# The opening of a hybrid decoder block: two projection units from un-normalised rows, in a written order

## The chip, the cores and the metric

The kernel runs on one core of a Trainium2 chip. The metric is the device time of one execution in microseconds (us); lower is better. The engines are TensorE (PE in the profile, its weight loads PEld), VectorE (DVE), ScalarE (ACT), GpSimd (POOL) and SyncE (SP), whose queue issues every DMA here.

## The reference, cut to what matters

One layer on 2048 positions of 1024 channels in float32: a norm, one combined input projection, two token mixers side by side (gated linear attention and a short gated convolution), an output projection, and a gated feed-forward part. The change concerns the norm and the first columns of the input projection.

```python
h = rmsnorm(x, norm1_g)                 # x * rsqrt(mean(x*x) + eps) * g, per position
proj = h @ w_in                         # columns: q, k, v, g, a (gate rank 16), conv B, C, h
q, k = p_q * DK ** -0.5, p_k            # 4 heads of 64
gate_logits = p_a @ w_gate_up + b_gate  # the forget gate, from the 16 columns a
log_a = log_sigmoid(gate_logits) / 16
```

The norm multiplies each position by one factor, so (x * g) @ w times the position's factor is the same as rmsnorm(x, g) @ w.

## The kernel before, in words

**Layout.** Activations lie transposed: channels on 128 partitions, positions along the free axis, in blocks of 512 positions (block j = 0 and 1 make the first half, 2 and 3 the second). A matmul has a 128x128 piece of weights and 128x512 positions. Every operand of a matmul is split into two float32r parts: hi, which ScalarE copies, and the remainder lo, which VectorE subtracts (`split`, L162 to L165). A product of two split operands is three matmuls: hi by hi, lo by hi, hi by lo.

**Units.** The input projection has 12 units for each half. A unit has 256 columns of `w_in`, so with two blocks of positions and two halves of channels a 2x2 by 2x2 block product. From unit 2 on it is done with seven products in place of eight (`PRODUCTS`, L36): weights A11, S1, S2, A12, S3, S4, A22 against activations B11, T1, T2, B21, T3, B22, T4, where S1 to S4 are sums and differences of weight quarters and T1 to T4 those of the normalised activations (`unit`, L452). Each product is 12 matmuls. The results accumulate in PSUM banks that are used on: the first product's bank `oa` is copied out into c11, takes the third product, is copied into c12, takes the fifth, is added into c22 and takes the seventh. The mixtures of the weights are made by GpSimd (L430 to L432, L437). Four buffers hold split weights, two hold raw weights, 28 hold operands, and eight PSUM banks serve all.

**The opening.** `first_loads` (L567) loads block 0's rows in halves, unit 0's four weight quarters, block 1's rows, and block 1 already transposed (`xt`). TensorE turns block 0's rows (32 transposes, L599), ScalarE takes their squares (L595). The squares' sums give one factor for each position by logarithm, exponential and a Newton step (`rsqrt`, L167); `rows_rstd` (L540) copies each factor over 128 columns (L552), and TensorE turns that (four transposes, L555) into a bank that holds the factors along the free axis. `scaled` (L613) multiplies a turned block by gain and factors, and the result is split. `build_first` (L322) does units' first work: for j = 0 and 1 and for each of 8 channel groups k, one normalised operand and six matmuls (two result rows, L362 to L364). `plain_unit` (L385) does unit 1 with the plain eight block products. Units 0 and 1 together take 192 matmuls. `differences` (L366) makes T1 to T4 from the normalised operands, which are overwritten.

**The gate.** `gate` (L691) multiplies 16 columns of `w_in` with the block: 32 matmuls into one bank (L702), then copies of it (a_sb, L713 to L715), the second factor `wgu_sb`, four matmuls (L724) and `forget_gate` (L730) with four running sums on VectorE each time. It is background work: a list of generators from which `tick` takes one step after each product (L241), paced by `pause(8)`. Behind it stand row statistics of the second half (`row_stats`, L517) and `h1_ahead` (L646), which prepares that half's operands.

**What sets the order.** The program is written in one order, and a scheduler with a timeline moves instructions of an engine past each other where dependences allow; `tc.issue_after` forces one instruction behind another. Within an engine the built order is strict. SP's DMAs are issued in its queue's order.

Of the kernel before, what the change touches and what calls it, by code (L numbers as in the profile page):

```python
# [52 lines left out]
def tile_hymba_block(ctx, tc, x, xt, win, wa, wgu, wout, wffn, wdown, wdown_first, small, out):  # L53
# [98 lines left out]
    second_weights, unit_splits, unsplit = [], [], []  # L152
# [8 lines left out]

    def split(src, hi, lo):  # L162
        last_hi[:] = [act.activation(hi, src, AF.Copy)]  # L163
        last_lo[:] = [dve.tensor_tensor(lo, src, hi.bitcast(F32), ALU.subtract)]  # L164
        return last_lo[0]  # L165
# [95 lines left out]
    def pause(n):  # L261
        for _ in range(n):
            yield

# [57 lines left out]
    def build_first(quad, w):  # L322


        ops = {b: [] for _, b in PRODUCTS}
        h, o = {}, {}
        quarters = ("A11", "A12"), ("A21", "A22")
        los = []

        def weight(n, i, *marks):  # L330
            with ExitStack() as stack:
                for m in (last_exp[0], *marks):
                    stack.enter_context(tc.issue_after(m.ins))
                w[n] = weight_quarter(first_raw[0][:, i, :])

        weight("A11", 0, last_copy[0])
        los.append(last_lo[0])
        for j in range(2):
            for r in range(2):
                o[r, j] = bank()  # L340
            for k in range(KD):
                with tc.issue_after(los[-2 if len(los) > 2 else -1].ins):
                    h[k, j] = quad(k, j)
                if (j, k) == (0, 0):
                    weight("A21", 3, last_scaled[0])
                x = opp.tile([P, 2, PB], F32R, name="op", tag="op")
                los.append(split(h[k, j][:], x[:, 0, :], x[:, 1, :]))
                hi = last_hi[0]
                if j == 0 and k in (1, 2):
                    weight(*(("A12", 1), ("A22", 2))[k - 1], los[-1])  # L350
                if j == 0 and k < PT:
                    with tc.issue_after(hi.ins):
                        row_squares(k)
                if (j, k) == (0, PT + 2):
                    rbs[1] = rows_rstd(squares[1][:, :, 0])
                name = ("B11", "B12")[j] if k < 4 else ("B21", "B22")[j]
                ops.setdefault(name, []).append(x)
                c = slice(k % 4 * P, (k % 4 + 1) * P)
                for r in range(2):
                    q = w[quarters[r][k // 4]]  # L360
                    with tc.issue_after(last_turn[0].ins):
                        pe.matmul(o[r, j][:], q[:, 0, c], x[:, 0, :], start=k == 0, stop=False)  # L362
                    pe.matmul(o[r, j][:], q[:, 1, c], x[:, 0, :], start=False, stop=False)
                    pe.matmul(o[r, j][:], q[:, 0, c], x[:, 1, :], start=False, stop=k == KD - 1)  # L364

        def differences(wanted):  # L366
            for n, y, a, b in (
                ("T1", (0, 0), (0, 1), (0, 0)), ("T2", (0, 0), (4, 1), (0, 0)),
                ("T3", (0, 1), (4, 1), (0, 1)), ("T4", (0, 0), (4, 0), (0, 0)),
            ):  # L370
                for k in range(4 if n in wanted else 0):
                    yy, aa, bb = [h[k + dk, j] for dk, j in (y, a, b)]
                    with tc.issue_after(los[-1].ins):
                        dve.tensor_tensor(yy[:], aa[:], bb[:], ALU.subtract)
                    o = opp.tile([P, 2, PB], F32R, name="op", tag="op")
                    ops[n].append(o)
                    if n == "T4":
                        unsplit.append((yy, o))
                    else:
                        with behind(second_weights):  # L380
                            split(yy[:], o[:, 0, :], o[:, 1, :])

        return ops, [(r, j, o[r, j], True) for j in range(2) for r in range(2)], differences

    def plain_unit(src, ops, differences):  # L385

        raw = raw_weights(src)
        us, columns = [], (("B11", "B21"), ("B12", "B22"))
        w = [weight_quarter(raw[:, i, :]) for i in (0, 1, 3, 2)]
        second_weights[:] = last_hi + last_lo  # L390
        differences(("T1", "T2", "T3"))
        for r in range(2):
            for j in range(2):
                o = bank()
                for i, n in enumerate(columns[j]):
                    for k in range(4):
                        product_step(o, w[2 * r + i], ops[n], k, i == 0)
                    tick()
                us.append((r, j, settled(o, True), False))
        return us  # L400

    halves = []

    def weight_quarter(src):

        n = src.shape[-1]
        if halves:
# [44 lines left out]
    def unit(src, ops, into=None, onto=None, raw=None):  # L452
# [19 lines left out]
        def plus(t, o):  # L472
            dve.tensor_tensor(t[:], o[:], t[:], ALU.add)  # L473
            return t
# [913 lines left out]
```

## Time and profile before

| what | value |
| --- | --- |
| timed runs | median 2060.56 us (2060.33, 2060.56, 2063.51) |
| the profiled execution | span of 2059.3 us; the page lists no other time of it |
| PE busy | 2018.4 us, 98% |
| DVE busy | 1425.3 us, 69% |
| ACT busy | 959.7 us, 47% |
| POOL busy | 859.8 us, 42% |
| HBM | 274.98 MB read, 144.70 MB written |

The span runs from the first to the last instruction on the core. A row of a timeline gives start, duration, engine, line, operation, written and read tile, shapes and count, and in brackets the idle time before it with what ended it. A row of a table by stage gives the stage, its length, and for PE, PEld, DVE, ACT and POOL the busy time and the count. A matmul's duration overlaps its neighbours'; the time from one start to the next is its cost in a stream.

### The profile page before, as it was taken

The page shows a single profiled execution, that of the slowest core. Times are in us where ns is not written, and L with a number is a line of the kernel's source. Part 1 is how long each engine was busy: PE and PEld are TensorE (multiplying, and loading weights), DVE is VectorE, ACT ScalarE, POOL GpSimd, SP SyncE. Part 2 cuts the span into 40 slices and gives each one's busy share as a digit, 9 for nine tenths or more (in the row PEclk, how much of TensorE's full clock was granted, in tenths as well). Part 3 has the DMA queues.
Part 4 walks back from the last instruction along what each step waited for, and adds up shares of the span by engine and source line. Part 5 has one row for each costly group of instructions (what it writes and reads, how often), then busy time and mean ns, then how long its engine had stood idle before and what let it go on. Part 6 is the DMA issues. An engine that isn't in the chain of part 4 may idle for free.

```text
span 2059.3 us, 27063 instructions
## 1 busy us (share of the span) xinstructions
PE 2018.4 (98%) x9229; PEld 1657.3 (80%) x9229; DVE 1425.3 (69%) x2128; ACT 959.7 (47%) x1918; POOL 859.8 (42%) x622
## 2 busy tenths in 40 slices
PE   7999999999999999999999999999999999999997
PEld 6877888787888888888888878787888888878786
DVE  8789686559743886676675676767666666667774
ACT  6655365765542344444444452334434444453344
POOL 0345322122102564464564345534644544435544
PEclk9999999999999999999999999999999999999998
DMA  6378485416586873545454676476444434586653
GB/s 229 116 274 278 159 319 165 143 67 194 190 296 246 311 254 130 198 181 207 156 185 143 241 264 254 185 282 257 163 164 167 175 140 169 179 309 223 234 217 126
DMA packets 188729, 421.47 MB, mean 205 GB/s; under 512 B 19792, under 2 KB 65072, under 8 KB 178992
## 3 DMA queue, kind: packets, MB, share of 16 engines
q1 hardware_dynamic: 188592, 419.76, 57.2%
q8 instruction: 72, 1.18, 0.2%
q14 instruction: 65, 0.53, 0.1%
HBM read 274.98 MB, written 144.70 MB: 204 GB/s over the span
## 4 chain that ended last, share of the span: by engine, by line
PE 84%; DVE 7%; DMA 4%; ACT 3%; issue 1%; POOL 1%; SPq 0%; DVEq 0%; ACTq 0%; POOLq 0%
PE mm L448 24%; PE mm L449 23%; PE mm L450 23%; PE mm L945 3%; PE mm L948 3%; PE mm L946 3%; DVE wq L164 2%; DVE op L164 1%; DMA op<-sa_B 1%; DMA op<-sa_T 1%; PE a_ps L702 1%; ACT wq L163 1%; DMA siT<-lo 1%; PE o_ps L869 1%; PE o_ps L871 1%
## 5 line engine op out<-in xcount | busy, mean ns | idle before, releaser
L448 PE MATMUL mm<-op,wq 128*128 128x512 f32 x2499 | 973.7, 392 | 10.3 <-ACT c L480 5.3
L449 PE MATMUL mm<-op,wq 128*128 128x512 f32 x2499 | 972.5, 390 | 1.6 <-DVE op L164 1.6
L450 PE MATMUL mm<-op,wq 128*128 128x512 f32 x2499 | 961.3, 390 | 2.6 <-DVE wq L164 2.3
L164 DVE TENSOR_TENSOR wq<-raw,wq 128x512 fp32r<-128x512 f32 (+2 forms) x626 | 508.9, 818 | 262.6 <-ACT wq L163 260.0
L163 ACT ACTIVATE wq<-raw 128x512 fp32r<-128x512 f32 (+2 forms) x626 | 364.9, 589 | 585.6 <-PE mm L450 447.9
L448 PEld LDWEIGHTS mm<-op,wq 128*128 128x128 f32 x2499 | 468.9, 188 | 114.9 <-ACT c L480 8.0
L450 PEld LDWEIGHTS mm<-op,wq 128*128 128x128 f32 x2499 | 469.1, 188 | 103.8 <-DVE wq L164 6.1
L449 PEld LDWEIGHTS mm<-op,wq 128*128 128x128 f32 x2499 | 469.3, 188 | 99.1 <-DVE op L164 3.7
L432 POOL TENSOR_TENSOR raw<-s,raw 128x512 f32<-128x512 f32 (+2 forms) x97 | 133.3, 1374 | 518.5 <-DVE wq L164 474.7
L430 POOL TENSOR_TENSOR s<-raw 128x512 f32<-128x512 f32 (+2 forms) x97 | 127.4, 1313 | 247.5 <-DMA raw<-in_wffn_dram 90.7
L473 DVE TENSOR_TENSOR c<-mm,c 128x512 f32<-128x512 f32 x198 | 135.8, 686 | 72.7 <-PE mm L450 70.9
L473 DVE TENSOR_TENSOR y<-mm,y 128x512 f32<-128x512 f32 x185 | 126.9, 687 | 83.3 <-PE mm L450 82.9
L437 POOL TENSOR_TENSOR raw<-raw 128x512 f32<-128x512 f32 (+2 forms) x97 | 120.6, 1244 | 126.7 <-DVE wq L164 126.7
L927 POOL TENSOR_TENSOR ssx<-ssx,q 128x512 f32<-128x512 f32 x52 | 77.4, 1504 | 158.8 <-ACT q L926 158.5
L431 POOL TENSOR_TENSOR raw<-raw 128x512 f32<-128x512 f32 (+2 forms) x97 | 137.3, 1416 | 4.9
L480 ACT ACTIVATE c<-mm 128x512 f32<-128x512 f32 x198 | 116.1, 587 | 11.1 <-PE mm L450 9.3
L945 PE MATMUL mm<-op,wq 128*128 128x512 f32 x256 | 100.9, 395 | 0.0
L946 PE MATMUL mm<-op,wq 128*128 128x512 f32 x256 | 99.7, 389 | 0.0
L163 ACT ACTIVATE wq<-s 128x512 fp32r<-128x512 f32 (+2 forms) x97 | 56.9, 587 | 89.3 <-PE mm L450 85.4
L164 DVE TENSOR_TENSOR wq<-s,wq 128x512 fp32r<-128x512 f32 (+2 forms) x97 | 82.6, 852 | 2.8 <-ACT wq L163 2.1
L164 DVE TENSOR_TENSOR op<-op 128x512 fp32r<-128x512 f32 x94 | 76.8, 844 | 4.7 <-ACT op L163 4.6
L948 PE MATMUL mm<-op,wq 128*128 128x512 f32 x256 | 79.8, 390 | 0.0
(204 smaller groups left out, 1807.6 us busy)
## 6 DMA issues: line engine op xcount, KB each, us to landing
raw<-in_wffn_dram SPq DMA_DIRECT2D x44, 1024.0 KB, 6.5
sa_B<-so SPq DMA_DIRECT2D x47, 512.0 KB, 4.2
op<-sa_B SPq DMA_DIRECT2D x47, 512.0 KB, 7.1
raw<-in_win_dram SPq DMA_DIRECT2D x23, 1024.0 KB, 5.4
sa_T<-so SPq DMA_DIRECT2D x44, 512.0 KB, 4.5
op<-sa_T SPq DMA_DIRECT2D x44, 512.0 KB, 6.9
raw<-in_wdown_dram SPq DMA_DIRECT2D x24, 768.0 KB, 5.8
sx<-y SPq DMA_DIRECT2D x48, 256.0 KB, 4.0
```

The costliest lines, as they stand in the source:

```text
L163: last_hi[:] = [act.activation(hi, src, AF.Copy)]
L164: last_lo[:] = [dve.tensor_tensor(lo, src, hi.bitcast(F32), ALU.subtract)]
L430: pool.tensor_tensor(s1, a21, a22, ALU.add)
L431: pool.tensor_tensor(a21, a11, a21, ALU.subtract)
L432: pool.tensor_tensor(a11, s1, a11, ALU.subtract)
L448: pe.matmul(o[:], wh, xh, start=first and k == 0, stop=False, skip_group_check=True)
L449: pe.matmul(o[:], wh, xl, start=False, stop=False, skip_group_check=True)
L450: return pe.matmul(o[:], wl, xh, start=False, stop=k == n - 1, skip_group_check=True)
L473: dve.tensor_tensor(t[:], o[:], t[:], ALU.add)
L945: pe.matmul(o[e, j][:], wh, m[:, 0, :], start=k == 0, stop=False)
L946: pe.matmul(o[e, j][:], wh, m[:, 1, :], start=False, stop=False)
L948: pe.matmul(o[e, j][:], wl, ops[k][j][:, 0, :], start=False, stop=k == KD - 1)
```

## The change

The opening is written anew as one function, `opening`, whose instructions on ScalarE and VectorE stand in a given order (`queued` forces each behind the one before it on its engine; a remainder is queued after the next hi part).

- Block 0 of units 0 and 1 is computed from the turned rows times the gain, without the position's factor: `taken` splits straight from PSUM (ScalarE scales by the gain; VectorE's remainder is one scalar_tensor_tensor). The factor is applied to the results on VectorE (`out` with j = 0).
- Their second block follows, from normalised operands, then the gate's 32 matmuls, then unit 2.
- Twelve matmuls on a tile of ones are issued before the transposes.
- Loads are in another order: unit 0's first two weight quarters come ahead of the second halves of the rows, unit 1's weights are loaded in quarters, and block 0's lower channel groups are also loaded transposed (four more loads).
- Normalised operands of block 0 are made after those of block 1; T1 comes ahead of the gate's product, T2 ahead of unit 2's weights, T3 and T4 among them (`between`).
- Unit 2's mixtures of weights are made by VectorE in the given order, and its additions are issued behind the last instruction of this order (`given`).
- `pause`, `build_first`, `plain_unit`, `first_loads` and `build_h` go; `rows_rstd` keeps the variant without tables, in two steps.

```diff
+    def queued(eng, issue):
+        with behind([tails[eng]] if eng in tails else []):
+            tails[eng] = issue()
+        return tails[eng]
+    def catch_up():
+        while late:
+            last_lo[:] = [queued(dve, late.pop(0))]
...
+        last_hi[:] = [queued(act, lambda: act.activation(hi, src, AF.Copy, scale=scale))]
+        catch_up()
...
+                lambda: dve.scalar_tensor_tensor(lo, src, gain, top, ALU.mult, ALU.subtract)
...
+        def mix(*args):
+            if ordered:
+                queued(dve, lambda: dve.tensor_tensor(*args))
+            else:
+                pool.tensor_tensor(*args)
...
+        w = unit_weights(src, raw, between)
+        given = []
+        if ordered:
+            catch_up()
+            ordered.clear()
+            given += last_lo
...
-            dve.tensor_tensor(t[:], o[:], t[:], ALU.add)
+            with behind(given):
+                dve.tensor_tensor(t[:], o[:], t[:], ALU.add)
...
+        for t in range(PT):
+            fetch_rows(0, t, 0)
+        fetch_w(0, 0)
+        fetch_w(0, 3)
+        for t in range(PT):
+            fetch_rows(0, t, 1)
+        fetch_w(0, 1)
+        fetch_w(0, 2)
+        fetch_w(1, 0)
...
+        def taken(k):
+            x_op[k] = opp.tile([P, 2, PB], F32R, name="op", tag="op")
+            split_in_order(xts[k][:], x_op[k][:, 0, :], x_op[k][:, 1, :], col(C_G1 + k))
...
+            if j:
+                queued(act, lambda: act.activation(c[:], acc[:], AF.Copy))
+            else:
+                queued(dve, lambda: dve.tensor_tensor(c[:], acc[:], rb0[:], ALU.mult))
...
+        for _ in range(12):
+            pe.matmul(warm[:, 0:P], ones[:], ones[:], start=True, stop=True)
+        turned(0)
+        for t in range(PT):
+            square(0, t, 0)
+        weight(0, "A11")
+        taken(0)
+        weight(0, "A21")
+        taken(1)
+        square(0, 0, 1)
+        taken(2)
+        square(0, 1, 1)
+        taken(3)
+        for k in range(3):
+            for r in range(2):
+                mark = column(0, 0, r, k)
+        with behind([mark]):
+            turned(1)
+        weight(0, "A12")
+        square(0, 2, 1)
+        taken(4)
+        weight(0, "A22")
+        taken(5)
+        square(0, 3, 1)
+        est = estimate(0)
+        taken(6)
+        for k in range(3, 6):
+            for r in range(2):
+                mark = column(0, 0, r, k)
+        weight(1, "A11")
+        rep = spread(*est)
+        taken(7)
+        rb_ps, done = turn(rep, mark)
...
+        after = []
+        steps = gate(0, ops, mark, after)
+        next(steps)
+        made("T2")
+        between = [
+            [lambda: out(1, 1, 0)], [lambda: out(1, 1, 1)], [partial(made, "T3"), lambda: after.extend(last_hi)], [],
+            [partial(made, "T4")],
+        ]
+        return ops, raw2, between, steps
```

More of the change, by code (lines that the diff above doesn't have):

```diff
@@ L320, in combine @@
             yield
[L322 to L400, printed above, removed]
@@ L1250, in tile_hymba_block @@
     act.preload_act_table_set("natural_log_exp_and_others")
-    first_loads()
-    for i in range(6):
-        load(carry[16 * i : 16 * i + 16, 0:2, :], wgu[0:16, :].rearrange("p (h c) -> p h c", c=P))
-    ops, first, differences = build_h()
+    ops, raw, between, steps = opening()
     hurry.append(True)
```

374 lines of the change are left out of this document (266 added, 108 removed).

## The prediction

> **What bounds the kernel now.** I read the totals first, then the busy time by stage (columns: busy time and count of PE, PEld, DVE, ACT and POOL, then granted clock, DMA share, GB/s), then the timeline of the opening, engine by engine.
>
> ```profile
> span 2059.3 us, 27063 instructions
> PE 2018.4 (98%) x9229; PEld 1657.3 (80%) x9229; DVE 1425.3 (69%) x2128; ACT 959.7 (47%) x1918; POOL 859.8 (42%) x622
> ```
>
> ```profile
> 0.00:28.30 28.30, 17.06 (x75) 13.96 (x76) 19.27 (x47) 18.98 (x42) 1.11 (x7) 0.94 0.88 315
> 28.30:111.00 82.70, 82.70 (x365) 67.91 (x363) 66.88 (x119) 52.18 (x112) 23.24 (x11) 1.00 0.39 137
> 111.00:210.00 99.00, 95.47 (x419) 77.28 (x419) 86.22 (x128) 51.60 (x101) 53.23 (x36) 1.00 0.79 270
> 210.00:2059.00 1849.00, 1823.15 (x8375) 1498.20 (x8373) 1252.95 (x1836) 836.92 (x1664) 782.19 (x569) 1.00 0.57 203
> ```
>
> TensorE is the bound: busy 2018.4 of 2059.3 us. Of the 40.9 us in which it is idle, 28.3 - 17.06 = 11.2 lie ahead of 28.3 us, none from there to 111, 3.5 from 111 to 210 and 25.9 in the rest, where TensorE's order is the same in both built programs but for a few places. In the second stage 365 matmuls fill 82.7 us: 0.2266 us each. So the change can win only in the first 28 us, and it loses wherever it opens a gap behind them. Why TensorE starts late:
>
> ```profile
> 5.08 1.94 PE L599 MATMUL xt<-ident,xr 128*128 128x128 f32 x8 [5.08 <-DMA xr<-in_x_dram]
> 7.29 4.04 PE L599 MATMUL xt<-ident,xr 128*128 128x128 f32 x24 [0.28 <-DMA xr<-in_x_dram]
> 13.32 0.64 PE L555 MATMUL rb_ps<-ident,rep 128*128 128x128 f32 x4 [1.98 <-DVE rep L552]
> 16.39 0.73 PE L362 MATMUL mm<-op,wq 128*128 128x512 f32 x1 [2.42 <-ACT op L163]
> ```
>
> ```profile
> 7.33 0.63 ACT L595 ACTIVATE q<-xr 128x512 f32<-128x512 f32 x1 [0.94 <-DMA xr<-in_x_dram]
> 7.87 0.19 ACT L595 ACTIVATION_READ_ACCUMULATOR q<-xr 128x1 f32 x1
> 7.99 0.63 ACT L595 ACTIVATE q<-xr 128x512 f32<-128x512 f32 x1
> ...
> 11.88 0.21 ACT L169 ACTIVATE rl<-msq 128x4 f32<-128x4 f32 x1 [0.43 <-DVE msq L543]
> 12.12 0.21 ACT L170 ACTIVATE ry<-rl 128x4 f32<-128x4 f32 x1
> 12.23 2.18 ACT L163 ACTIVATE wq<-raw 128x512 fp32r<-128x512 f32 x4
> 14.31 0.58 ACT L611 ACTIVATE rb<-rb_ps 128x512 f32<-128x512 f32 x1
> 15.70 0.63 ACT L163 ACTIVATE op<-h 128x512 fp32r<-128x512 f32 x1 [0.81 <-DVE h L615]
> ```
>
> The transposes of the rows run from 5.08 us as the rows land (ScalarE's third square waits until 7.33, the fourth follows at 7.99). The first matmul comes at 16.39: it needs an operand that is already normalised, so it stands behind all squares, logarithm and exponential (11.88, 12.12), the row factors and the first split (15.70). The weights' splits, at 12.23, are earlier.
>
> **The change, step by step.** Times are on the trace's axis; durations and pitches are those of the rows; the orders on the engines are those of the two built programs.
>
> ```profile
> 12.35 0.16 DVE L175 TENSOR_TENSOR rl<-ry 128x4 f32<-128x4 f32 x1 [0.51 <-ACT ry L170]
> 12.55 0.16 DVE L176 SCALAR_TENSOR_TENSOR rl<-rl,msq 128x4 f32<-128x4 f32 x1
> 12.75 0.16 DVE L177 SCALAR_TENSOR_TENSOR msq<-rl,ry 128x4 f32<-128x4 f32 x1
> 12.95 0.63 DVE L552 COPY rep<-msq 128x128 f32<-128x128 f32 x4
> 13.49 0.69 DVE L164 TENSOR_TENSOR wq<-raw,wq 128x512 fp32r<-128x512 f32 x1
> ```
>
> ```profile
> 14.00:16.00 2.00, 0.00 (x0) 0.00 (x0) 1.26 (x3) 1.19 (x3) 0.00 (x0) 1.00 1.04 414
> 16.00:18.00 2.00, 1.61 (x4) 1.33 (x5) 1.90 (x4) 1.62 (x4) 0.00 (x0) 0.62 1.01 396
> 18.00:20.00 2.00, 2.00 (x6) 1.51 (x6) 1.96 (x4) 2.00 (x5) 0.00 (x0) 0.53 1.06 388
> 20.00:22.00 2.00, 2.00 (x11) 1.62 (x10) 2.00 (x4) 2.00 (x4) 0.00 (x0) 1.00 1.05 386
> ```
>
> *First matmul.* The operands are now the turned rows times the gain, split straight from PSUM, and two quarters of the weights are fetched in places 5 and 6, behind the four half rows. At 414 GB/s 256 KB take 0.63 us; the fourth is there by 7.99, so these land at about 8.6 and 9.3. ScalarE's splits follow each other at (2.18 - 0.63)/3 = 0.52, its squares at 7.99 - 7.33 = 0.66. The fourth square is over at 8.7; then weight 8.7, operand 9.2 to 9.8, second weight 9.7, second operand 10.2. VectorE's remainders (0.69 each) start behind them at 9.3, 9.9, 10.6 and 11.2. First matmul at 9.85, 6.5 us earlier. 18 matmuls then run almost without a gap: 14.1.
>
> *Up to the first row factors.* 16 more transposes follow. Four turns took 0.64 us with the drain of the last (13.32); I take 2.0 for the 16, which gives 16.1 (2.6 at most). The fifth operand is split from 15.85, then a weight, the sixth operand (0.52 each) and the last square with its sum (0.66 + 0.19): 18.15. Sum and mean 0.4, logarithm and exponential 0.21 each with gaps: 19.05. The seventh operand's split and remainder: 20.4. Newton's three steps at 0.2, the copies from 21.0, the first turn 0.37 later (12.95 to 13.32): 21.35. TensorE has 18 matmuls meanwhile, to 20.2, and **waits 1.15 us**.
>
> ```profile
> 27.95 0.64 PE L555 MATMUL rb_ps<-ident,rep 128*128 128x128 f32 x4 [1.48 <-DVE rep L552]
> 28.35 0.48 PE L362 MATMUL mm<-op,wq 128*128 128x512 f32 x1
> ```
>
> What follows the turns starts 0.40 behind their start, at 21.8; the 12 last matmuls of unit 0's first block end at 24.5. Before: at 28.35 eight turns and 36 of these 48 matmuls were done, and 12 more make 31.07. After: 24.5 with four turns, the other four are due later: 25.15. **Gain of the opening 5.9 us.**
>
> *To the gate's product.* Still 144 matmuls and four turns: 24.5 + 32.6 + 0.64 = 57.8, if they are fed.
>
> ```profile
> 28.63 1.41 DVE L615 SCALAR_TENSOR_TENSOR h<-h,sml,rb_ps 128x512 f32<-128x512 f32 x2 [0.42 <-PE rb_ps L555]
> ...
> 41.09 4.90 DVE L374 TENSOR_TENSOR h<-h 128x512 f32<-128x512 f32 x8
> ...
> 63.66 1.23 DVE L164 TENSOR_TENSOR wq<-raw,wq 128x512 fp32r<-128x512 f32 x1 [1.85 <-ACT wq L163]
> ```
>
> ```profile
> 69.43 3.01 PE a_ps L702 x13
> ...
> 75.18 4.42 PE a_ps L702 x19
> ```
>
> A normalised operand costs VectorE 0.67 + 0.60 = 1.27 us (pitches in the rows at 28.63 and 41.09); TensorE spends 6 x 0.2266 = 1.36 on it. The first is complete at 35.9, TensorE comes at 36.0: it holds, by 0.1 at first and by more later. The operands of the first block and T1 are ready at 55.2. The gate's 32 matmuls take 3.01 + 4.42 = 7.4, as before: 65.2.
>
> *The new wait.* Unit 2 has seven products of 12 matmuls, 2.72 us each. The last, A22 with T4, accumulates into a bank that the addition into c22 must first have read, and this addition is now made to issue behind A22's remainder, the end of the given order. In the built order of before, the next unit's first product and the start of its second stand ahead of this one and hide the addition; in that of after nothing does. ScalarE's queue is in order, and c22's copy in it waits for the second product: 65.2 + 5.45 + 0.25 = 70.9. Behind it stand two squares and then T3's third split, which ends at 73.3. From there VectorE has 18 instructions of 0.60 in its given order, the addition into c22 the last: 10.8 us, with 0.6 of waits for ScalarE's splits 84.7. TensorE is there at 65.2 + 6 x 2.72 = 81.5. **Cost 3.2 us** (1.5 if half of ScalarE's queue and VectorE's waits dissolve, 4.5 if GpSimd, below, collides with it).
>
> *After it.* The forget gate's work on VectorE now starts behind this wait, some 4 us later against TensorE's place than before, and ScalarE's copy of unit 2's last result holds its queue until that product is done. Laid against TensorE's through units 3 and 4, VectorE's order delivers remainders 0.05 to 0.8 us before they are needed. Nothing is left for a collision with GpSimd:
>
> ```profile
> 54.12 8.83 POOL L432 TENSOR_TENSOR raw<-s,raw 128x512 f32<-128x512 f32 x1 [20.35 <-DVE wq L164]
> 63.03 1.30 POOL L430 TENSOR_TENSOR s<-raw 128x512 f32<-128x512 f32 x1
> ```
>
> A remainder took 1.23 us in place of 0.69 beside GpSimd's addition at 63.03, and GpSimd's own took 8.83 in place of 1.30 beside a busy VectorE. Four additions that each cost VectorE 0.54 make 2.2. Bounds 0 and 2.2; I take 1.0, the middle, since TensorE's wait in unit 2 lets VectorE catch up.
>
> *Costed at nothing.* The twelve warming matmuls lie ahead of 5.08, where TensorE is idle (eight cold transposes took 1.94, so 12 make 2.9 us if it were not). VectorE's extra work (eight remainders of un-normalised operands, four scalings of outputs, unit 2's four mixtures from GpSimd, less four copies: 12 x 0.60 to 0.67, about 7.7 us) fits into the 82.7 - 66.9 = 15.8 us that it had free up to 111; without that cover all of it would come out on TensorE. SP issues four more loads of 256 KB (2.5 us), wanted only at 45 us.
>
> **Sum:** -5.9 + 3.2 + 1.0 = -1.7 us on the span of 2059.3, so 2057.6. The timed runs' median, 2060.56, stands 1.26 above that span, which I carry over: **2058.9**.
>
> **The rivals.** *The wait in unit 2 is mostly hidden* and VectorE keeps up, with 1.2 us left of both: -5.9 + 1.2, so 2055.9. For it: ScalarE's chain is laid from rows of other stages; against it: the instruction order shows the dependence. *The clock is cold* at the first matmuls: the stages at 16 and 18 us show half the clock (0.62, 0.53) after TensorE had idled, and full clock from 20. If the warming matmuls and transposes don't count, some 3.4 us at half rate cost 1.7: 2060.6. Against it: TensorE is busy for most of each stretch from 1.2 us on. The Trainium skill, "TensorE: Matmul & The Clock Gate", Part 1, says that the gate watches a free-running window of 3413 ns, so that the slow stretch ends at another place from run to run; the trace's slow rows agree with that length. *The opening starts later than laid*, because a weight's landing or the row factors come 3 us late: -2.9 + 4.2, so 2061.9. *VectorE becomes the bound through units 3 and 4* (slower): GpSimd's eight mixtures of these units each hold it for their 1.3 us while it is the late one, 10.4 us, less some 2 that it makes up: -5.9 + 3.2 + 8.4, so 2066.3. It decides once VectorE's work for a unit exceeds the unit's 84 x 0.2266 = 19.0 us; from 111 to 210 it was busy 86.2 of 99, or 16.6 for each unit, which speaks against it. The Trainium skill, "SBUF — State Buffer", section "SBUF: two separate sides", calls the ports that these two engines share an exclusive lock for a whole instruction; the 1.23 and the 8.83 agree.
>
> **How the numbers follow.** Forecast 2058.9 with chance 0.45, hidden wait 0.22, cold clock 0.12, late opening 0.08, VectorE as the bound 0.13. This measurement can tell about 0.2%, or 4.1 us, from no change: 2056.4 to 2064.7 counts as the same. So faster 0.22, same 0.65, slower 0.13. The range takes in the forecast with its bounds and the first three rivals and leaves out the last: from 2055.4 (the hidden wait with 0.5 us less of it) to 2063.1 (the late opening with 2.2 in place of 1.0).
>
> **What would show it.** The first matmul near 9.9 us; a gap of about 1 us before the first turns of row factors; TensorE without a gap from 22 to 81 us; a gap of about 3 us ahead of unit 2's last product, ended by VectorE's addition into c22; small gaps, ended by VectorE's remainders, up to 112. If the granted clock is half at 10 us, or the gap in unit 2 is missing or exceeds 5 us, the sum is wrong there.

## The result and the profile after

| | before | after |
|---|---|---|
| time, median of 6 runs | 2061.31 us (2059.86 to 2063.51) | 2067.57 us (2064.27 to 2070.10) |
| ratio | | 1.0029, 95% interval 1.0017 to 1.0041 |
| profiled execution: time, span | 2060.56, 2059.3 us | 2064.27, 2062.5 us |

The changed kernel is slower, by about 6 us. The forecast was 2058.9, faster than before, with a range up to 2063.1: it had the wrong sign, and the measured time lies above the range. The profiled execution of the changed kernel is the shortest of its six; the traces of the experiments repeat what it shows up to 213 us, but only in part what it gains after that.

First the page's totals and the busy time by stage (PE, PEld, DVE, ACT, POOL with counts, then granted clock, DMA share, GB/s), cut at the same times as before the change:

```profile
span 2062.5 us, 27137 instructions
```

```profile
0.00:28.30 28.30, 23.72 (x114) 19.55 (x115) 14.42 (x33) 18.39 (x40) 1.11 (x7) 0.94 0.92 320
28.30:111.00 82.70, 78.88 (x342) 64.13 (x341) 76.12 (x137) 53.32 (x112) 9.44 (x7) 0.98 0.41 134
111.00:210.00 99.00, 93.61 (x406) 74.47 (x405) 83.24 (x129) 51.42 (x102) 53.24 (x36) 1.00 0.80 270
210.00:2062.00 1852.00, 1827.88 (x8397) 1502.18 (x8395) 1256.87 (x1846) 837.90 (x1670) 784.59 (x569) 1.00 0.57 203
```

Up to 28.3 us TensorE did 114 matmul records where it did 75; 24 of the 114 are the warming ones (the twelve leave two records each). In the second stage, where it had no idle time at all, it now idles 82.70 - 78.88 = 3.8 us, and VectorE's busy time there rose from 66.88 to 76.12. To see where the time went I numbered TensorE's matmuls from the end of both traces (the changed one has 24 more in all, at its start) and took, for the same place of the order, the start after less the start before:

| place, time before | 34 us | 79 | 89 | 93 | 129 | 138 | 164 | 178 | 192 | 199 | 206 | 220 | 553 | 2050 |
|---|---|---|---|---|---|---|---|---|---|---|---|---|---|---|
| after less before, us | -3.2 | -3.6 | +0.8 | +1.4 | +4.2 | +3.7 | +0.1 | +0.1 | +2.2 | +4.6 | +5.8 | +6.0 | +6.0 | +3.2 |

A gain of 3.6 us at the opening; a loss of 5.0 around 84 to 91 us; 2.3 more by 138 (only 0.6 of it by 112, where the difference is +2.0); 3.6 given back by 164, where the kernel before has gaps of its own; then 5.9 lost from 178 to 220. From there to 553 us nothing changes.

The opening, TensorE's timeline after (start, length, engine, line, operation, count, idle time before it and what ended it):

```profile
1.12 4.88 PE L709 MATMUL warm<-ones 128*128 128x128 f32 x24 [1.12 <-DVE ones L79]
5.84 2.49 PE L598 MATMUL xt<-ident,xr 128*128 128x128 f32 x16
10.33 0.51 PE L686 MATMUL mm<-op,wq 128*128 128x512 f32 x1 [2.00 <-ACT op L178]
...
13.97 0.63 PE L687 MATMUL mm<-op,wq 128*128 128x512 f32 x1
...
15.81 0.40 PE L686 MATMUL mm<-op,wq 128*128 128x512 f32 x1
...
23.86 0.64 PE L652 MATMUL rb_ps<-ident,rep 128*128 128x128 f32 x4 [1.12 <-DVE rep L642]
```

ScalarE's first split, of the weight that the first matmul needs:

```profile
9.07 0.63 ACT L178 ACTIVATE wq<-raw 128x512 fp32r<-128x512 f32 x1 [0.56 <-DMA raw<-in_win_dram]
```

The first matmul stands at 10.33 (16.39 before). Between about 12 and 15.5 us a matmul takes 0.63 instead of 0.39 us and they start 0.43 apart instead of 0.23: half clock. The turns of the row factors come at 23.86.

Unit 2's end, TensorE and then VectorE:

```profile
83.83 0.39 PE L414 MATMUL mm<-op,wq 128*128 128x512 f32 x1
87.57 0.76 PE L412 MATMUL mm<-op,wq 128*128 128x512 f32 x1 [3.35 <-DVE c L443]
88.14 0.63 PE L413 MATMUL mm<-op,wq 128*128 128x512 f32 x1
...
90.63 0.39 PE L413 MATMUL mm<-op,wq 128*128 128x512 f32 x1
```

```profile
83.43 0.68 DVE L677 TENSOR_TENSOR h<-h 128x512 f32<-128x512 f32 x1
84.03 1.47 DVE L182 TENSOR_TENSOR op<-h,op 128x512 fp32r<-128x512 f32 x2
85.42 0.69 DVE L182 TENSOR_TENSOR wq<-raw,wq 128x512 fp32r<-128x512 f32 x1
86.14 1.89 DVE L443 TENSOR_TENSOR c<-mm,c 128x512 f32<-128x512 f32 x3
```

The wait that was forecast is there, with its length (3.35 us) and its releaser, and matmuls at half clock follow it up to 90.3. VectorE runs without a break ahead of it: differences, remainders, then the additions.

How full VectorE is shows in windows of 60 to 90 us and three later ones, first of the kernel before, then after:

```profile
60.00:90.00 30.00, 30.00 (x133) 24.59 (x132) 16.67 (x25) 16.48 (x34) 10.57 (x7) 1.00 0.29 101
93.00:112.00 19.00, 18.79 (x83) 15.24 (x82) 17.81 (x44) 15.43 (x41) 3.05 (x2) 1.00 0.58 201
141.00:178.00 37.00, 34.36 (x149) 27.45 (x148) 32.14 (x36) 17.51 (x31) 25.42 (x17) 1.00 0.98 343
178.00:213.00 35.00, 34.33 (x150) 27.75 (x150) 34.49 (x46) 18.10 (x39) 14.67 (x11) 1.00 0.70 221
```

```profile
60.00:90.00 30.00, 26.65 (x112) 21.38 (x111) 27.71 (x42) 18.62 (x38) 3.57 (x3) 0.95 0.20 60
93.00:112.00 19.00, 18.53 (x82) 14.93 (x81) 18.79 (x39) 16.74 (x41) 5.60 (x4) 1.00 0.61 197
141.00:178.00 37.00, 37.00 (x165) 30.64 (x164) 29.02 (x37) 18.87 (x32) 23.79 (x17) 1.00 0.94 318
178.00:213.00 35.00, 30.13 (x125) 22.53 (x124) 33.83 (x44) 17.93 (x39) 19.19 (x12) 1.00 0.75 245
```

From 60 to 90 us VectorE (the third pair) was busy 16.67 of 30 us before and is busy 27.71 now. In the kernel before that was no idle time thrown away: there VectorE ran ahead. I call *lead* the time from the end of a weight's remainder to the first matmul that reads it (the n-th remainder laid beside the n-th product in the trace). Before, the last four weights of unit 2 had leads of 13.3, 14.2, 14.3 and 12.0 us; after, 5.7, 1.4, 2.1 and 2.5. What held VectorE back there in the kernel before is seen in its longest wait and in ScalarE's just before it:

```profile
75.88 0.69 DVE L164 TENSOR_TENSOR wq<-raw,wq 128x512 fp32r<-128x512 f32 x1 [4.99 <-ACT wq L163]
```

```profile
75.22 0.63 ACT L163 ACTIVATE wq<-raw 128x512 fp32r<-128x512 f32 x1 [4.57 <-PE mm L450]
```

VectorE waited for the hi part of a weight, and ScalarE could write that only when TensorE had done a product: the split weights were as far ahead as their buffers allow. This lead is spent by the end of unit 3, whose seven weights have leads from 7 us down to about 4 before, and from 3 to 6 after. From unit 5 on the two kernels have much the same, between about 1 and 8 us.

### The profile page after: what moved, and what is told of

Same layout as the page of the kernel before. It is cut to its first block, busy times and chain, and to the rows that moved or that the text cites. A ratio compares the mean times of both kernels' runs of the same rounds, so it can differ in the third digit from the quotient of the medians.

```text
span 2062.5 us, 27137 instructions
## 1 busy us (share of the span) xinstructions
PE 2024.1 (98%) x9253; PEld 1660.3 (81%) x9253; DVE 1430.6 (69%) x2140; ACT 961.0 (47%) x1922; POOL 848.4 (41%) x618
## 4 chain that ended last, share of the span: by engine, by line
PE 86%; DVE 7%; DMA 2%; ACT 2%; issue 1%; POOL 1%; SPq 0%; DVEq 0%; ACTq 0%; POOLq 0%
PE mm L412 24%; PE mm L414 24%; PE mm L413 24%; PE mm L1131 3%; PE mm L1132 3%; PE mm L1134 3%; DVE wq L192 2%; DMA op<-shT 1%; PE a_ps L890 1%; PE mm L688 1%; PE mm L686 1%; PE mm L687 1%; PE o_ps L1055 1%; PE o_ps L1057 1%; DVE op L192 1%
## 5 line engine op out<-in xcount | busy, mean ns | idle before, releaser
L412 PE MATMUL mm<-op,wq 128*128 128x512 f32 x2467 | 962.6, 393 | 14.9 <-ACT c L450 6.8
L413 PE MATMUL mm<-op,wq 128*128 128x512 f32 x2467 | 960.4, 390 | 0.3 <-DVE op L192 0.2
L414 PE MATMUL mm<-op,wq 128*128 128x512 f32 x2467 | 949.6, 390 | 4.3 <-DVE wq L192 4.2
L192 DVE TENSOR_TENSOR wq<-raw,wq 128x512 fp32r<-128x512 f32 (+2 forms) x612 | 495.3, 814 | 255.0 <-ACT wq L191 252.5
L191 ACT ACTIVATE wq<-raw 128x512 fp32r<-128x512 f32 (+2 forms) x612 | 355.6, 587 | 575.8 <-PE mm L414 441.3
L412 PEld LDWEIGHTS mm<-op,wq 128*128 128x128 f32 x2467 | 463.3, 188 | 120.0 <-ACT c L450 10.4
L414 PEld LDWEIGHTS mm<-op,wq 128*128 128x128 f32 x2467 | 463.3, 188 | 105.5 <-DVE wq L192 8.5
L413 PEld LDWEIGHTS mm<-op,wq 128*128 128x128 f32 x2467 | 463.7, 188 | 95.6 <-DVE op L192 1.8
L386 POOL TENSOR_TENSOR raw<-s,raw 128x512 f32<-128x512 f32 (+2 forms) x96 | 124.1, 1293 | 503.5 <-DVE wq L192 465.3
L1131 PE MATMUL mm<-op,wq 128*128 128x512 f32 x256 | 100.9, 395 | 0.0
L1132 PE MATMUL mm<-op,wq 128*128 128x512 f32 x256 | 99.7, 390 | 0.0
L1134 PE MATMUL mm<-op,wq 128*128 128x512 f32 x256 | 79.7, 390 | 0.0
L1326 POOL TENSOR_TENSOR y<-x,y 128x512 f32<-128x512 f32 x32 | 53.7, 1678 | 44.7 <-DVE y L443 40.4
```

The costliest lines, as they stand in the source:

```text
L386: pool.tensor_tensor(*args)
L412: pe.matmul(o[:], wh, xh, start=first and k == 0, stop=False, skip_group_check=True)
L413: pe.matmul(o[:], wh, xl, start=False, stop=False, skip_group_check=True)
L414: return pe.matmul(o[:], wl, xh, start=False, stop=k == n - 1, skip_group_check=True)
L1131: pe.matmul(o[e, j][:], wh, m[:, 0, :], start=k == 0, stop=False)
L1132: pe.matmul(o[e, j][:], wh, m[:, 1, :], start=False, stop=False)
```

## The experiments

Every time is the median of 4 to 12 runs, beside the kernel before on the same chip.

**1 to 4: the forced wait, the later h1 operands, the warming.** The first theory was that three separate things lose the time: the order behind the remainder (*wait*), the later start of the second half's operands h1, whose first difference on GpSimd came at 141.1 us instead of 133.0 (*late mixes*), and the cold clock.

```diff
 e1:             ordered.clear()
-            given += last_lo
+            pass
 e2:                 dve.tensor_copy(rep[:, t, :], y[:, t : t + 1].to_broadcast([P, P]))
-        yield
         rb.append(bank("rb_ps"))
 e3:
-        warm = bank("warm")
-        for _ in range(12):
-            pe.matmul(warm[:, 0:P], ones[:], ones[:], start=True, stop=True)
```

> The changed kernel, with the additions of unit 2 no longer placed behind the last remainder of its weights (the list that forces it is left empty). The changed kernel stood 6.3 us over the kernel before. Theory 'wait': the gap of 3.35 us before A22's product (83.84 to 87.57) goes, and with it the half clock at 87.1 to 90.6 that follows it; the matmul that stood 0.8 us later than before at 89 us stands about 3.6 us earlier, and all of the 4.4 us reach the end: about 1.9 us over the kernel before. Rival 'swallowed': at 164 to 178 us both kernels stood level (0.1 us apart) although they were 4 us apart just before, so a later wait levels them; the gap goes, but the end stays within 1.5 us of the changed kernel, about 6 us over the kernel before.

> The changed kernel, with the row factors of blocks 2 and 3 made in one background step each, as before, not in two (one yield of two left out). Theory 'late mixes': the two more steps start the h1 mixes on GpSimd 8 to 10 us later (first one at 141.1 against 133.0, last at 199.0 against 189.3), so they run beside units whose VectorE work they stretch to 1.77 us a piece, and this makes the 5.8 us lost between 178 and 213 us: the mixes end near 189 us, the loss there falls to under 2 us, and the kernel stands about 2 us over the kernel before (4 us under the changed kernel). Rival 'debt': the loss comes from VectorE work carried over from units 2 to 4, wherever the mixes stand: still 5 us or more over the kernel before.

> The changed kernel without the 12 small warming matmuls ahead of the first transposes. In the changed kernel they run from 1.12 to 6.00 us and push the first transposes from 5.08 to 5.84. Theory 'landing': the first product waits for weight A11 to land (9.05 us), for ScalarE's copy of it (9.07) and for the first operand (op hi at 9.61), so the transposes' 0.8 us are cover and the first matmul stays within 0.3 us of 10.33; the transposes run at half clock from 5.1 and the clock windows move by some us; end within 1 us of the changed kernel. Rival 'warm': without them the first products run at half clock for one window of 3.4 us more, 1.7 us later by 20 us.

> The edits of e1_no_given and e2_one_step together. If 'wait' and 'late mixes' both hold and their losses are apart in time, the two gains add: 8 us under the changed kernel, about 2 us under the kernel before, with neither the gap at 84 us nor the loss between 178 and 213 us. If the early gain is levelled by a later wait (rival 'swallowed'), the time is that of e2_one_step alone to within 1 us.

| | median | kernel before | ratio, 95% interval |
|---|---|---|---|
| e1, additions not placed behind the remainder | 2066.20 | 2061.54 | 1.0022, 1.0013 to 1.0032 |
| e2, one step per block | 2068.12 | 2061.54 | 1.0029, 1.0019 to 1.0038 |
| e3, no warming matmuls | 2067.79 | 2061.54 | 1.0023, 1.0012 to 1.0035 |
| e4, e1 and e2 | 2066.04 | 2061.54 | 1.0026, 1.0017 to 1.0035 |

None brings the loss back. In e1 the gap does not go, it shrinks by 0.6 us and changes its releaser (TensorE's timeline):

```profile
86.79 0.50 PE L412 MATMUL mm<-op,wq 128*128 128x512 f32 x1 [2.33 <-ACT wq L178]
88.01 0.79 PE L414 MATMUL mm<-op,wq 128*128 128x512 f32 x1 [0.44 <-DVE wq L182]
```

and this is why, on VectorE and then on ScalarE:

```profile
84.86 0.69 DVE L677 TENSOR_TENSOR h<-h 128x512 f32<-128x512 f32 x1
85.47 0.69 DVE L443 TENSOR_TENSOR c<-mm,c 128x512 f32<-128x512 f32 x1
86.07 1.29 DVE L182 TENSOR_TENSOR op<-h,op 128x512 fp32r<-128x512 f32 x2
87.27 0.69 DVE L182 TENSOR_TENSOR wq<-raw,wq 128x512 fp32r<-128x512 f32 x1
```

```profile
85.58 0.63 ACT L178 ACTIVATE op<-h 128x512 fp32r<-128x512 f32 x1 [0.57 <-DVE h L677]
86.12 0.61 ACT L178 ACTIVATE wq<-raw 128x512 fp32r<-128x512 f32 x1
```

The additions now come earlier, and what stood behind them comes later: T4's last difference ends at 85.55 us, ScalarE's splits of T4 and of A22 follow it, and A22's remainder ends at 87.96, not 86.11. The order decides only which of the results that hang on VectorE is the last one. So "wait" falls as a cause. In e2 TensorE loses nothing from 164 to 206 us (6.2 us behind the kernel before at 164 and from 178 to 192, 6.6 at 206), but it has already lost the same by 164: "late mixes" falls as well. e3's first matmul came at 9.99 us, as "landing" said, and it ends where the changed kernel ends; its opening has gained 2.8 us by 43 us where the changed kernel's has gained 3.6. On the clock the rival "warm" was right, though it came to 0.8 us, not 1.7 (TensorE's timeline of e3):

```profile
15.86 0.63 PE L686 MATMUL mm<-op,wq 128*128 128x512 f32 x1
16.29 0.51 PE L687 MATMUL mm<-op,wq 128*128 128x512 f32 x1
16.64 0.39 PE L686 MATMUL mm<-op,wq 128*128 128x512 f32 x1
```

Without the warming its matmuls start about 0.43 us apart from the first one up to 16.3 us, so the half clock lasts some 6 us here and 3.41 in the changed kernel. (The trace's clock rows begin only at 16.54 us in e3, so this is read from the matmuls.)

**5: VectorE work added to the kernel before.** New theory (*stock*): VectorE is what runs short, and the kernel before gets through because of the lead that it has built by the end of unit 2.

```diff
                     differences(("T4",))
+                    spare = bt("g1")
+                    for _ in range(26):
+                        dve.tensor_tensor(spare[:], unsplit[-1][0][:], unsplit[-1][0][:], ALU.add)
```

> The kernel before, with 26 additions of 128x512 on VectorE that feed nothing, placed after unit 1 (about 63 to 85 us; 26 x 0.69 = 17.9 us of VectorE). There VectorE stands idle for 9.65 us of 63 to 76, and unit 2's weights are ready 8 to 14 us before their products (lead: end of the remainder to the first matmul that reads it), against 1.4 to 5.7 us in the changed kernel. Theory 'stock': the kernel before owes its even run through units 3 to 8 to that lead; 17.9 - 9.65 = 8.3 us of it are eaten, unit 2's last products come down to leads of 4 to 6 us, and units 3 to 8 lose what the changed kernel loses there: 3 to 6 us over the kernel before. Rival 'covered': a lead of 14 us swallows 8.3 us, and the time stays within 1 us of the kernel before; then the changed kernel's loss has another cause than VectorE's state at the end of unit 2.

2067.64 against 2061.83, ratio 1.0034 (1.0021 to 1.0047): a loss of the size that the theory says, or a little more. Windows of this kernel:

```profile
60.00:90.00 30.00, 30.00 (x133) 24.61 (x132) 27.53 (x40) 14.37 (x31) 10.20 (x5) 1.00 0.28 103
93.00:112.00 19.00, 16.97 (x72) 13.12 (x72) 19.00 (x36) 12.67 (x31) 5.23 (x4) 1.00 0.49 159
```

VectorE is as full from 60 to 90 us as in the changed kernel, and TensorE does not notice it there. It pays from 93 to 112, where VectorE is busy 19.00 of 19.00 us and TensorE waits 2 us, and more just behind; the place that lies at 112 us in the kernel before has slipped by 4.8 us against the one at 93. The theory's place was not quite right: the last four weights of unit 2 still have leads of about 9 to 12 us (4 to 6 expected), and it is unit 3's that are down to 2.5 to 4.7. That VectorE's idle time ahead of 90 us is needed later is shown with nothing of the change in the kernel. But e5 loses nothing more from 112 to 553 us; what the changed kernel loses after 178 us it does not repeat.

**6 and 7: work given back to GpSimd.**

```diff
 e6:
-            queued(dve, lambda: dve.tensor_tensor(y[:], a[:], b[:], ALU.subtract))
+            eng = pool if n in ('T3', 'T4') else dve
+            queued(eng, lambda: eng.tensor_tensor(y[:], a[:], b[:], ALU.subtract))
 e7:
-            if ordered:
+            if False:
                 queued(dve, lambda: dve.tensor_tensor(*args))
```

> The changed kernel, with the eight differences of T3 and T4 made on GpSimd instead of VectorE: 8 x 0.68 = 5.5 us off VectorE in unit 2, where VectorE is busy 9.7 of 10 us and GpSimd 0.7. A difference on GpSimd takes about 1.3 us beside a VectorE that leaves it room (mixes of weights: 1.29 to 1.62 us), once 8.8 us beside one that doesn't. Theory 'VectorE debt': A22's product starts at 84.0 to 85 (not 87.57), the half clock at 87 goes, the leads in units 3 to 8 grow by 2 to 5 us, and the kernel comes to 2 to 0 us over the kernel before, 4 to 6 us under the changed kernel. Rival 'starved': GpSimd gets its turns late beside a saturated VectorE, T4 comes later than now, and the time is that of the changed kernel or up to 3 us over it.

> The changed kernel, with the four mixes of unit 2's weights on GpSimd as in the kernel before, not in VectorE's order: 4 x 0.69 = 2.8 us off VectorE, the first three of them early (their raw weights have landed before VectorE comes to them). Theory 'VectorE debt': the gap before A22's product falls from 3.35 to about 0.6 us and the half clock after it goes; 2 to 4 us under the changed kernel, if later units keep the gain; unit 2's S weights gain lead. Rival 'levelled': the gap shrinks but units 6 to 9 lose as much more, and the end moves by less than 1.5 us. Rival 'starved': GpSimd's mixes beside a full VectorE come late, S1 waits, and the time rises.

e6: 2070.63 against 2061.83, ratio 1.0042 (1.0028 to 1.0056), so the "starved" rival, up to 3 us over the changed kernel (the intervals of the two overlap). Its rows on GpSimd and on VectorE at the same time:

```profile
52.34 9.40 POOL L678 TENSOR_TENSOR h<-h 128x512 f32<-128x512 f32 x4 [50.53 <-DVE h L678]
```

```profile
58.03 3.79 DVE L182 TENSOR_TENSOR wa_sb<-wa,wa_sb 128x64 fp32r<-128x64 f32 x3
...
70.62 1.77 DVE L384 TENSOR_TENSOR s<-raw 128x512 f32<-128x512 f32 x1
```

Four differences took GpSimd 9.40 us, and beside them three small remainders, 0.5 us in the changed kernel, took VectorE 3.79, and an addition of 0.69 took 1.77. VectorE's busy time from 60 to 90 us rose to 29.26 us though it had fewer instructions (36 for 42). e7: 2067.02 against 2061.83, ratio 1.0027 (1.0018 to 1.0035); the matmuls on both sides of the gap start 3.0 us apart instead of 3.7, and the intervals can't tell it from the changed kernel: not the 2 to 4 us of "VectorE debt", but its rival "levelled". 2.8 us of work taken off VectorE's order freed it for only 1.2 us from 60 to 90 us (busy 26.52 for 27.71), and shortened the gap by 0.7.

**8 and 10, 11: h1 later.** Is the loss after 141 us that of h1 meeting short leads?

```diff
-            in_turn(steps, row_stats(2), row_stats(3)), unhurried(), h1_ahead(),
+            in_turn(steps, row_stats(2), row_stats(3)), unhurried(), (None for _ in range(10)), h1_ahead(),
```

> The changed kernel, with ten empty background steps ahead of the h1 operands of the second half (blocks 2 and 3), so that their VectorE work (16 foldings, 16 remainders) and GpSimd's 16 mixes start some 50 us later, when the weights' leads have grown back to 6 or 7 us (unit 10). Theory 'stock': the loss between 141 and 213 us comes because this work meets short leads (2 to 5 us); started with leads of 7 us it costs TensorE under 2 us: 3 to 5 us under the changed kernel, 1 to 3 us over the kernel before. Rival 'throughput': VectorE is over-full wherever the h1 work lies, its loss of about 5 us only moves to later units: within 1.5 us of the changed kernel. Second rival: the later start pushes gated attention's steps past the end of the half and costs time there, up to 10 us more.

> The changed kernel with four empty background steps (not ten) ahead of the h1 operands of the second half: they start about 22 us later. With ten, TensorE lost nothing between 93 and 206 us (it came from 2.5 us behind the kernel before to 1.8 us ahead) and then 27 us between 206 and 360 us, where h1 met the convolution and gated attention. Theory 'stock': with four the leads have grown to 6 us when h1 starts, and it still ends ahead of gated attention; 2 to 4 us under the changed kernel. Rival 'throughput': the h1 work runs into the convolution's units (units 8 to 10, eight foldings of 1 us each), the loss moves there: level with the changed kernel or up to 6 us over it.

> A candidate: the changed kernel with unit 2's mixes on GpSimd (0.5 us under the changed kernel alone), unit 2's additions free of the remainder (1.4 us under it alone) and four empty steps ahead of h1. Theory 'VectorE debt': 2.8 us less VectorE work and an earlier addition shrink the gap at 84 us from 3.35 to about 1 us, and the half clock goes; with what four steps give, 2 to 5 us under the changed kernel, so within 2 us of the kernel before on either side. Rival 'levelled': no better than the best of its parts, 1 to 1.5 us under the changed kernel.

e8, windows:

```profile
141.00:178.00 37.00, 37.00 (x165) 30.66 (x164) 14.48 (x20) 14.62 (x26) 10.33 (x8) 1.00 0.24 86
178.00:206.00 28.00, 28.00 (x129) 23.09 (x128) 23.20 (x33) 13.14 (x29) 9.72 (x7) 1.00 0.35 107
206.00:360.00 154.00, 135.97 (x623) 106.54 (x622) 119.27 (x174) 76.63 (x169) 57.19 (x38) 0.96 0.82 281
```

Without h1, TensorE has no idle time from 141 to 206 us and VectorE is half empty up to 178, so h1's work is what the stretch is short of. Which part of that work, this run does not tell: besides VectorE's, GpSimd's fell from 23.79 to 10.33 us from 141 to 178 and the loads from 318 to 86 GB/s. But put later it meets the convolution and gated attention: from 206 to 360 us TensorE is idle for 18 us (it was busy all 154 us there in the kernel before), and with half-clock stretches it loses 27 us. The whole: 2087.01 against 2061.83, ratio 1.0125 (1.0111 to 1.0139). Four steps (e10): 2074.36 against 2061.50, ratio 1.0061 (1.0049 to 1.0073); the candidate e11 (e1, e7 and four steps): 2073.27, ratio 1.0056 (1.0044 to 1.0068). So e8's second rival is right in kind, at about twice its "up to 10 us", and e10's "throughput" holds with 6.6 us over the changed kernel by the ratios (up to 6 expected); a later h1 is no remedy.

**9 and 12: VectorE's work left out.** The subtractions of T3 and T4 are skipped, so two products use other operands; no other engine's work changes, but ScalarE's splits of T3 and T4 no longer wait for the subtractions either.

```diff
-            queued(dve, lambda: dve.tensor_tensor(y[:], a[:], b[:], ALU.subtract))
+            if n in ("T1", "T2"): queued(dve, lambda: dve.tensor_tensor(y[:], a[:], b[:], ALU.subtract))
             final(n, k, y)
```

> The changed kernel with the eight subtractions of T3 and T4 left out (the operands T3 and T4 are split from the minuends' tiles as they are, so the two products use other numbers): 8 x 0.68 = 5.5 us off VectorE in unit 2, with nothing put on GpSimd and every other engine's work kept. Theory 'VectorE debt': A22's product no longer waits (under 0.5 us at 84 us), no half clock at 87 us, so the matmul at 89 us stands 3.6 us earlier than before, not 0.8 later; the leads at the end of unit 2 grow from 1.4-2.5 us to 4-8 us, and the stretch to 213 us gives back at most half of it: 4 to 7 us under the changed kernel, about level with the kernel before. Rival 'levelled': the opening's gain is kept to 90 us and lost by 213 us all the same, because the h1 work bounds that stretch: within 2 us of the changed kernel.

> The edits of e9_skip_T34 (the subtractions of T3 and T4 left out, so two products use other numbers) and e2_one_step (row factors of blocks 2 and 3 in one step each) together. e9 came level with the kernel before (+0.3 us), but in its trace TensorE still went from 4.0 us ahead of the kernel before at 171 us to 1.5 us behind at 220, while e2 lost nothing there and 2 to 3 us between 129 and 165 us. Theory 'place of h1' (a second cause beside VectorE's debt): with both, the loss after 171 us is gone, that between 129 and 165 us stays at 2 to 3 us, and the kernel ends 2 to 4 us under the kernel before. Rival 'h1 costs the same anywhere': what is saved after 171 us is lost ahead of it, and the end is within 1.5 us of e9, level with the kernel before.

e9: 2061.85 against 2061.50, ratio 1.0003 (0.9994 to 1.0011). 5.5 us of VectorE work less are worth about 5.4 us of time by the two ratios (0.0029 - 0.0003 of 2061.5; the ends of the two intervals lie 1.2 to 9.7 us apart), as "VectorE debt" said. The gap at 84 us is gone (window of e9; after: 0.65 of 4 us):

```profile
84.00:88.00 4.00, 4.00 (x19) 3.29 (x18) 3.51 (x4) 3.75 (x7) 2.38 (x3) 1.00 1.00 379
```

and TensorE stands 4.9 us ahead of the kernel before at 93 us (1.3 us more than the changed kernel's opening gained, since this trace has no half clock there). It does not keep that: it loses 4.6 by 112 us, behind a VectorE remainder, with a half-clock stretch behind the longer wait,

```profile
93.06 0.50 PE L414 MATMUL mm<-op,wq 128*128 128x512 f32 x1 [0.59 <-DVE wq L192]
101.12 0.50 PE L414 MATMUL mm<-op,wq 128*128 128x512 f32 x1 [2.33 <-DVE wq L192]
```

and 5.2 more from 178 to 220. The theory had at most half of the gain given back; all of it is, as the rival "levelled" had it, though from a better place. e12 (e9 with h1 in one step): 2064.34 against 2061.86, ratio 1.0007 (0.9998 to 1.0017). By the ratios 0.8 us from e9, by the medians 2.1, and not under the kernel before: "place of h1" falls for good, what is saved after 171 us is lost ahead of it.

## Why the prediction was wrong

**The step that failed** is the one costed at nothing: VectorE's extra 7.7 us "fits into the 82.7 - 66.9 = 15.8 us that it had free up to 111". Those 15.8 us were not free: they stand for VectorE having run ahead, up to 14 us on the weights of unit 2, and unit 3, where VectorE is nearly full (17.81 of 19 us from 93 to 112), lived on that lead. Nor was 7.7 all that was asked of them. By 28.3 us VectorE has done 14.42 us of work instead of 19.27, so 4.9 us came on top, and TensorE wants its operands 3.6 us earlier. As a sum up to 111 us it even fitted, since VectorE's busy time there rose by 9.2 us and left 6.6 idle; but from 60 to 90 us the idle time fell from 13.3 to 2.3, and there the wait opened. The runs agree that VectorE's amount of work sets the time: 5.5 us taken away came back as about 5.4 us (e9), and 17.9 us added to the kernel before made it as slow as the changed one (e5). Work given to GpSimd instead does not count in full: e7's 2.8 us freed VectorE for 1.2, and the time can't be told from the changed kernel's.

Term by term, on the profiled execution:

- **Opening, -5.9: measured -3.6.** First matmul 10.33 against 9.85, since ScalarE waited for the first weight until 9.07, not 8.7; the wait ahead of the first row factors was 1.12 us as forecast (1.15). Most of the rest is the clock: the rival "cold clock" had the right price (1.7 us), but as an alternative, where it came on top. Its condition, that the warming does not count, did not hold (e3); the half clock came behind the 2.00 us of idle time between transposes and first matmul. In the three traces of the same opening without a half-clock stretch (e9, e10, e11) the gain was 4.9, 5.3 and 5.4 us.
- **The new wait, +3.2: measured 3.35**, with the releaser as named. Missed: the half clock after it, 1.65 us more, for 5.0 in all (from -3.6 to +1.4 in the table). And its cause was put in the order "behind A22's remainder"; e1 shows that without this order most of the wait stays, and e9 that with 5.5 us less VectorE work it goes.
- **After it, +1.0, to 112 us: measured +0.6 there** (1.4 to 2.0), **but +4.6 by 213 us** (1.4 to 6.0), for which the sum had no term. "Remainders 0.05 to 0.8 us before they are needed" was a stretch with no room, and was priced as if only GpSimd's additions could disturb it. h1, whose foldings begin at about 130 us, was not in the sum.
- **"TensorE without a gap from 22 to 81 us"** held but for the row factors' wait; normalised operands kept up. The warming matmuls did cost: they took 4.88 us, not 2.9, and ran until 6.00, 0.8 us into the transposes, which had started at 5.08 before; on the other side, the opening without them (e3) gained 0.8 us less.
- **The rival on the other side**, VectorE as the bound, 2066.3 with a chance of 0.13, came nearest. It named the engine and the size, but not the place (units 3 and 4) and not the reason (GpSimd's mixtures): the loss lies in unit 2 and in units 3 to 9 up to 213 us, and taking unit 2's mixtures off VectorE's order (e7) changes little. It was argued down by an average, 16.6 us of VectorE for a unit of 19.0. The windows show that the average hid full stretches: 17.81 of 19 us from 93 to 112 and 34.49 of 35 from 178 to 213.

What stays open is the 5.9 us after 178, net 2.3 from 138 on. VectorE is full there in both kernels, and in the changed one TensorE's waits of 4.9 us from 178 to 213 are ended by VectorE's results for 2.7 us and by ScalarE's copies out of PSUM for 2.2. ScalarE in turn waited for GpSimd's mixtures. TensorE's waits from 88 to 215 us (total, times, longest; the first row has the 3.35 us of unit 2 in it), and ScalarE's longest:

```profile
PE mm L412 <- DVE c L443: 3.8, 2, 3.4
PE mm L412 <- ACT c L450: 3.2, 4, 1.1
PE mm L414 <- DVE wq L192: 2.7, 4, 1.0
```

```profile
179.54 0.63 ACT L191 ACTIVATE hi<-t 128x512 fp32r<-128x512 f32 x1 [5.98 <-POOL t L331]
```

How much of this is VectorE's work, how much GpSimd's and how much the loads of h1 is not shown. One folding waited 3.14 us for its load, and behind it VectorE was full (its timeline, and a window, of the changed kernel):

```profile
177.01 0.75 DVE L814 SCALAR_TENSOR_TENSOR h<-h,sml,rb_ps 128x512 f32<-128x512 f32 x1 [3.14 <-DMA h<-in_xt_dram]
```

```profile
190.00:210.00 20.00, 17.22 (x72) 12.89 (x72) 20.00 (x25) 8.23 (x19) 11.36 (x7) 1.00 0.71 231
```

The loads were not tried by themselves; e2 and e12 show only that moving h1 by two steps does not change the sum, and e9 that the stretch still loses time with 5.5 us less VectorE work ahead of it.

## What to carry to other kernels

Idle time of an engine is not free if the engine is idle because it has run as far ahead as its buffers let it: look at the lead of its results over their readers, not at its busy share, and at where that lead is spent. An earlier start of the busiest engine is then kept only if the engines that feed it can be earlier too: here 3.6 us were lost by 91 us, and in e9 4.9 by 112. And test a wait by its releaser: if the wait stays when the first releaser is moved, and ends on another result that hangs on the same engine, that engine's amount of work is the likelier cause than the order; taking work away, as in e9, then tests it.

## What the runs showed of the hardware

**The clock.** The half-clock stretches are 3.41 us long or twice that and lie on a grid of this step (12.04 and 87.14 in the changed kernel are 22 steps apart). I laid the idle times of TensorE on that grid in all 14 traces, from the first clock row of each up to 390 us: each half-clock stretch begins behind a step with at least 1.6 us of idle time; every step with over 1.9 us is followed by one; from 1.6 to 1.9 it went either way (1.63 in e12 did it, 1.73 in the kernel before didn't). So 2 us of idle time ahead of the first matmul cost 1.7 us more when they fall into one step (1.89 of them between 8.6 and 12.0 in the changed kernel), and nothing when an edge divides them (e10: 2.05 us idle, 1.5 in the fuller step, no half clock). The Trainium skill, "TensorE: Matmul & The Clock Gate", Part 1, has a window of 3413 ns that runs freely; the traces agree, and add that about half a window of idle time can be enough. Why a stretch sometimes lasts a second window, with 0.3 to 1.5 us of idle time in the first, they do not tell.

**VectorE beside GpSimd.** In e6 an addition of 0.69 us on VectorE took 1.77 beside GpSimd's differences, 1.1 more, and three small remainders 3.79 instead of 0.5, 1.1 more for each. The Trainium skill, "Perfetto Trace Analysis", section "Optimizing Scalar/DVE Operations", warns that moving work between these two might not help; e6 agrees: 5.5 us taken off VectorE left it busier from 60 to 90 us (29.26 for 27.71) and the kernel no faster.
